# A decoder trunk on one core: dense matmuls read their moved operand from two halves in turn

## The chip, the cores and the metric

The kernel runs on one core of one Trainium2 chip. The metric is the device time of the program in microseconds (us), median of several runs; lower is better. Five engines work side by side and meet by semaphores: TensorE (PE: matmuls, and PEld: the loads of the operand that is held in the array), VectorE (DVE), ScalarE (ACT), GpSimd (POOL) and SyncE (SP, which here only issues DMAs). A matmul holds one operand of up to 128 x 128 in the array (the held one, loaded ahead) and streams the columns of the other past it (the moved one); its result goes to a bank of PSUM, 512 float32 in each of 128 partitions, of which there are eight. DVE and ACT take results out of PSUM into SBUF (here called an evacuation).

## The reference, cut to what matters

```python
for l in range(DEPTH):                       # 2 layers, x is 512 tokens x 1024
    x = x + 0.5 * swiglu(rms_norm(x, ffn1_norm[l]), ffn1_w_in[l], ffn1_w_out[l])
    h = rms_norm(x, mix_norm[l]) @ w_mix_in[l]            # 1024 -> 3336
    ...                                                   # conv, HGRN2 and forgetting attention
    x = x + y @ w_mix_out[l]                              # 1024 -> 1024
    x = x + 0.5 * swiglu(rms_norm(x, ffn2_norm[l]), ffn2_w_in[l], ffn2_w_out[l])

def swiglu(h, w_in, w_out):                               # 1024 -> 2 x 2816 -> 1024
    gate, up = jnp.split(h @ w_in, 2, axis=-1)
    return (jax.nn.silu(gate) * up) @ w_out
```

Everything is float32.

## The kernel before

**Three products for one.** Each float32 operand is split into a rounded part (`hi`) and a rest (`lo`), both of a four-byte type that PE streams in one pass; a product is hi x hi + hi x lo + lo x hi. `mm3` (L408 to 422) issues these three matmuls (L413, L419, L420). The weights are split as they arrive: an ACT cast writes `hi`, a DVE subtraction `lo` (L398 and L401 in `parted`, L865 and L867 in `prepare`), both into a tile `hl`. The activations stand ready as pairs: `xh`, `xl` (normalised input, made in `norm_part`), `hh`, `hl` (hidden values), `yh`, `yl` (mixer output).

**Two kinds of matmuls.** The larger part of each feed-forward block is computed by a seven-product scheme on halves of the tokens (`halved`, planned in `plan`); its matmuls move 256 columns and go through `mm3` too. The rest is dense and moves 512 columns: with the features in the rows of the result, the 512 tokens are moved past a 128 x 128 block of weights; with the tokens in the rows (`tokens`, and the last output chunk), 512 columns of weights are moved past 128 tokens. These dense stages are:

- the entry of each feed-forward block (`cover`, L651 on): the first `covered` blocks of hidden features (6 in the first block, 4 in the others), for which PE has work while the normalisation and the operands of the seven-product scheme are prepared. The preparing steps are dealt out by the table `ENTRY`;
- its last chunk of w_out (`ffn`, second half), 6 rows of blocks; in the very last block it is done with the tokens in the rows, and the last quarter of the output in two half-wide pieces;
- the mixer: `features` for the HGRN inputs, `tokens` for the attention's q, k, v (`fox_qkv`, L1528 on), `features_steps` for the convolution (`conv_in`, `conv_out`), and the output projection (`most`, then a loop over `dg`).

All of them go through `stream_steps` (L428 on), which walks over the rows of the weights, two or more blocks of 128 at a time, and calls `mm3` for each job (a bank, a slice of weights). Two places issue the three products themselves: the opening of the program (`first`, L466) and the last rows of the first half of the output projection (`late`, L497).

**Banks and order.** `next4` gives two sets of four banks in turn, so that one set is evacuated while the next is filled. The order of PE's instructions is written out by hand through `follow`; DVE and ACT keep program order in the stages where their work is dealt.

**The evacuations** of dense results: the residual additions (L644 in `ffn`; L1210 `add` in `mix`; L633 for the output), the multiplication by the inverse norm (L667, L668 `clear`; L1124, L1126, L1142 in `mix`; L1255, L1272 in the convolution), a copy (L1254), and in `fox_qkv` the copies of q and k (L1567) and the split of v (L1578, L1579). Each reads one bank in order.

Of the kernel before, what the change touches and what calls it, by code (L numbers as in the profile page):

```python
# [26 lines left out]
T = 512  # L27
# [39 lines left out]
HD = 64  # L67
# [12 lines left out]
def plan(covered):  # L80
# [89 lines left out]
    for a, b, what in sorted(loose, key=lambda x: (x[1], x[0])):  # L170
# [8 lines left out]
    return seq, {  # L179
        n: [(w[0], w[1:]) for _, w in sorted(todo[n], key=lambda x: x[0])] for n in todo  # L180
    }


class Trunk:
# [223 lines left out]
    def mm3(self, acc, ah, al, bh, bl, first, last, parted=False, keep=False):  # L408

        nc = self.nc  # L410
        n = bh.shape[-1]
        for c in (slice(0, n // 2), slice(n // 2, n)) if parted else (slice(0, n),):
            i = nc.tensor.matmul(  # L413
                acc[:, c], ah, bh[:, c], start=first and c.start == 0, stop=False,
                skip_group_check=True,
            )
            if keep:
                self.follow("p", i)
        nc.tensor.matmul(acc, ah, bl, start=False, stop=False, skip_group_check=True)  # L419
        i = nc.tensor.matmul(acc, al, bh, start=False, stop=last, skip_group_check=True)  # L420
        if keep:
            self.follow("p", i)

# [4 lines left out]
    def stream_steps(  # L428
        self, jobs, parts_of, act, nk, mid=None, pre=None, deal=None, keep=False, lead=False,
        fine=False, deep=2, rowwise=False, late=False,  # L430
    ):

        k = 0
        while k < nk:
            kk = min(deep, nk - k)
            if callable(mid) and k == nk - 2:
                mid()
            st = None  # L450
            if pre is not None:

                if k == 0:
                    st = self.open_rows(parts_of(k, kk), kk)
                pre(k)
            if deal is not None:
                deal(k)
            skew = SKEW_MOVING if jobs[0][2] is not None and jobs[0][0].shape[-1] < T else 0
            if st is not None:

                def first(hi, lo):

                    ah, al = act(0)
                    for n, (w, x) in enumerate(((hi, ah), (lo, ah), (hi, al))):
                        for acc, cols, _ in jobs:
                            self.follow("p", self.nc.tensor.matmul(  # L466
                                acc, w[:, cols], x, start=n == 0, stop=False, skip_group_check=True
                            ))
                        if n == 0:
                            pre(k, None)  # L470

                self.between = first
            rows = self.granule(parts_of(k, kk), kk, pre is None, skew, deal is not None, st)
            if st is not None:
                self.first_rows = self.chain["v"]
            end = k + kk == nk
            order = (
                [(job, j) for job in jobs for j in range(kk)]
                if end and not rowwise or lead and k == 0
                else [(job, j) for j in range(kk) for job in jobs]  # L480
            )
            for n, ((acc, cols, toks, *more), j) in enumerate(order):
                if pre is not None and n == len(order) // 2:
                    pre(k, True)
                if fine and n == len(order) // 2:
                    yield
                if pre is not None and k + j == 0:
                    continue
                ah, al = act(k + j)
                hi, lo = rows[j]  # L490
                first, stop = k + j == 0 and not more, end and j == kk - 1
                if late and stop:

                    if acc is jobs[0][0]:
                        for i, (w, x) in enumerate(((hi, ah), (lo, ah), (hi, al))):
                            for acc, cols, _ in jobs:
                                self.follow("p", self.nc.tensor.matmul(  # L497
                                    acc, w[:, cols], x, start=False, stop=i == 2, skip_group_check=True
                                ))
                    continue  # L500
                if toks is None:
                    self.mm3(acc, hi[:, cols], lo[:, cols], ah, al, first, stop, False, keep)
                else:
                    self.mm3(
                        acc, ah[:, toks], al[:, toks], hi[:, cols], lo[:, cols], first, stop, False, keep
                    )
            k += kk
            yield
# [74 lines left out]
    def ffn(self, w_in, w_out, next_gain, covered, mean=None, begin=None, out=None):  # L583
# [5 lines left out]
        with tc.tile_pool(name=self.n("ffn"), bufs=1) as fp:  # L589
# [14 lines left out]
            for dg in range(2):  # L604
# [24 lines left out]
                if last:  # L629
                    for i in range(4):  # L630
                        o = self.xo[dg * 4 + i]
                        for bk, c in pieces[i]:
                            nc.vector.scalar_tensor_tensor(  # L633
                                out=o[:, c], in0=bk, scalar=0.5,
                                in1=xs[dg * 4 + i][:, c], op0=ALU.mult, op1=ALU.add,
                            )
                            nc.sync.dma_start(
                                out[0, spans[i], dg * T + c.start : dg * T + c.stop], o[:, c]
                            )
                    continue  # L640
                for i in range(4):
                    j = dg * 4 + i
                    xj = self.xT[:, j, :]
                    nc.vector.scalar_tensor_tensor(  # L644
                        out=xj, in0=banks[i], scalar=0.5, in1=xj,
                        op0=ALU.mult, op1=ALU.add,
                    )
                    if next_gain is not None:
                        self.norm_part(j, fp)

    def cover(self, fp, w_in, w_out, covered, mean, begin):  # L651
# [10 lines left out]
        def clear(t):  # L662

            gi = fp.tile([P, T], F32, tag="g2", name=self.n("gi"), bufs=2)
            ui = fp.tile([P, T], F32, tag="u2", name=self.n("ui"), bufs=2)
            pg, pu = tiles[t]
            V(nc.vector.tensor_mul(gi, pg, self.inv))  # L667
            V(nc.vector.tensor_mul(ui, pu, self.inv))  # L668
            values[t] = gi, ui

        def value(t):
# [387 lines left out]
    def mix(self, l, w, w_out, conv_w, out_gain, q_gain, k_gain, f_bias, next_gain, logits):  # L1059
# [3 lines left out]
        with tc.tile_pool(name=self.n("mix"), bufs=1) as mp:  # L1063
# [48 lines left out]
            with tc.tile_pool(name=self.n("hg"), bufs=1) as hp:  # L1112
# [8 lines left out]
                inv = self.inv  # L1121
                z, sg = pair(hp, "z"), pair(hp, "sg")
                for i in range(2):
                    nc.vector.tensor_mul(z[i], bz[i], inv)  # L1124
                for i in range(2):
                    nc.vector.tensor_mul(sg[i], bg[i], inv)  # L1126
                self.table(SILU)
                for i in range(2):
                    self.act(sg[i], sg[i], AF.Silu)
# [9 lines left out]
                )  # L1139
                bq = features([(H_Q, 256)], ("mm", "mm"))  # L1140
                for i in range(2):
                    nc.vector.tensor_mul(q[i], bq[i], inv)  # L1142

                bv = [self.bank(t) for t in ("mm", "sc", "sc", "mm")]
                self.stream(
# [29 lines left out]
            with tc.tile_pool(name=self.n("at"), bufs=1) as ap_:  # L1175
# [31 lines left out]
                    return lambda k: (self.yh[order[k0 + k]], self.yl[order[k0 + k]])  # L1207

                def add(j, bank):
                    nc.vector.tensor_add(self.xT[:, j, :], bank, self.xT[:, j, :])  # L1210

                def most():

# [36 lines left out]
    def conv_in(self, pool, i, px, pc, inv2, cw):  # L1250
        nc = self.nc
        u = pool.tile([P, T], F32, tag="t", name=self.n("cu"), bufs=self.tb)
        y = self.mp.tile([P, T], F32, tag=f"cyl{i}", name=self.n("cy"))
        nc.scalar.copy(y, px)  # L1254
        nc.vector.tensor_mul(u, pc, inv2)  # L1255
        nc.vector.tensor_mul(u, u, y)
        tap = lambda j: cw[:, 2 * j + i : 2 * j + i + 1]
        nc.scalar.activation(y, u, AF.Copy, scale=tap(2))
        nc.vector.scalar_tensor_tensor(
            out=y[:, 1:], in0=u[:, : T - 1], scalar=tap(1), in1=y[:, 1:], op0=ALU.mult, op1=ALU.add  # L1260
        )
        nc.vector.scalar_tensor_tensor(
            out=y[:, 2:], in0=u[:, : T - 2], scalar=tap(0), in1=y[:, 2:], op0=ALU.mult, op1=ALU.add
        )
        self.cy = getattr(self, "cy", {})
        self.cy[i] = y

    def conv_out(self, pool, i, pb):
        nc = self.nc
        y = self.cy[i]  # L1270
        u = pool.tile([P, T], F32, tag="t", name=self.n("cu"), bufs=self.tb)
        nc.vector.tensor_mul(u, pb, self.inv)  # L1272
        nc.vector.tensor_mul(u, y, u)
        self.yl[i] = self.mp.tile([P, T], F32R, tag=f"cyl{i}", name=self.n("cyl"))
        nc.scalar.copy(self.yh[i], u)
# [252 lines left out]
    def fox_qkv(self, mp, hp, tokens, half):  # L1528
# [34 lines left out]
        for hf in range(2):  # L1563
            qk = mp.tile([P, 4, 4, 2, HD], F32, tag="qk", name=self.n("qk"), bufs=2)
            banks = yield from beside(tokens((F_Q + 256 * hf, 256), (F_K + 256 * hf, 256)))
            for i, bank in enumerate(banks):
                nc.scalar.copy(  # L1567
                    qk[:, i].rearrange("p h w d -> p w h d"),
                    bank.rearrange("p (w h d) -> p w h d", w=2, h=4),
                )  # L1570
                later.append(lambda qk=qk, i=i: norm(qk, i))
            half.append(qk)
        V = mp.tile([P, 4, NH, 2, HD], F32R, tag="V", name=self.n("V"))
        half.append(V)
        for i, bank in enumerate((yield from beside(tokens((F_V, T), keep=True)))):
            src = bank.rearrange("p (h d) -> p h d", d=HD)
            sc = self.invc[:, i : i + 1]
            nc.scalar.activation(V[:, i, :, 0, :], src, AF.Copy, scale=sc)  # L1578
            nc.vector.scalar_tensor_tensor(  # L1579
                out=V[:, i, :, 1, :], in0=src, scalar=sc, in1=V[:, i, :, 0, :],  # L1580
                op0=ALU.mult, op1=ALU.subtract,
            )

    def fox_prep(self, pool, h, qk, g):
# [280 lines left out]
```

## Time and profile before

| what | value |
|---|---|
| median of 3 runs | 1821.0 us (1819.95 to 1823.05) |
| profiled execution, span from first to last instruction | 1816.5 us |
| median of the runs above that span | 4.5 us |
| PE busy | 1808.4 us, 100% of the span |
| DVE busy | 1431.7 us, 79% |
| ACT busy | 995.2 us, 55% |
| share of PE in the chain that ended last | 96% |
| granted TensorE clock, mean | 1.000 |

The profile is of one execution, whose own duration is known as its span; what lies around the span is taken from the difference to the median of the runs. Busy times of PE overlap: each record reaches from a matmul's start to the modelled end of its last column. How fast a stream of matmuls runs is therefore read from the distance of their starts.

### The profile page before, as it was taken

The numbers are of one execution on the slowest core, as the hardware profiler recorded it, in microseconds if no ns is written. First come the engines' busy times: TensorE is split into PE (matmuls) and PEld (weight loads), VectorE is DVE, ScalarE is ACT, GpSimd is POOL, SyncE is SP. The second block draws the span as 40 slices with busy tenths as digits, with TensorE's granted clock in tenths as the row PEclk, the third lists the DMA queues.
The fourth block names the chain that finished last, engine by engine and source line by source line (L and its number), as shares of the span: only waits on it lengthen the run. The fifth ranks groups of instructions, "written<-read, shape, count | busy, mean of one in ns | idle before, by whom it ended". The sixth has DMA issues, their size and how long they took to land.

```text
span 1816.5 us, 33373 instructions
## 1 busy us (share of the span) xinstructions
PE 1808.4 (100%) x13613; PEld 1656.6 (91%) x13613; DVE 1431.7 (79%) x1991; ACT 995.2 (55%) x1417; POOL 176.8 (10%) x174
## 2 busy tenths in 40 slices
PE   9999999999999999999999999999999999999999
PEld 7899999887788899999889999998878888999998
DVE  8889887678677898879678887876777778888883
ACT  5455555465665465555445555555656655555552
POOL 0011120100000101112001111201000001020210
PEclk9999999999999999999999999999999999999999
DMA  7658784343543867868276787923435438677762
GB/s 214 180 128 191 182 174 97 73 115 87 129 106 99 225 141 160 196 161 170 82 202 141 165 190 188 172 66 82 122 84 126 118 96 217 163 153 197 152 139 93
DMA packets 253114, 262.35 MB, mean 144 GB/s; under 512 B 23528, under 2 KB 232176, under 8 KB 252960
## 3 DMA queue, kind: packets, MB, share of 16 engines
q1 hardware_dynamic: 197104, 192.02, 35.9%
q0 software_dynamic: 55840, 68.19, 23.5%
q8 instruction: 107, 1.75, 0.4%
q14 instruction: 47, 0.39, 0.1%
q10 hardware_dynamic: 16, 0.00, 0.0%
HBM read 226.15 MB, written 2.17 MB: 126 GB/s over the span
## 4 chain that ended last, share of the span: by engine, by line
PE 96%; DVE 1%; DMA 1%; ACT 1%; issue 0%; SPq 0%; ACTq 0%; DVEq 0%
PE mm L413 15%; PE mm L420 14%; PE mm L419 14%; PE sc L413 6%; PE sc L420 6%; PE sc L419 6%; PE pt L413 6%; PE pt L420 6%; PE pt L419 6%; PE po L413 4%; PE po L419 4%; PE po L420 4%; PE sc L1641 1%; PE po L1696 1%; PE pt L1678 1%; DMA st<-in_ffn_w_in_dram 1%
## 5 line engine op out<-in xcount | busy, mean ns | idle before, releaser
L865 ACT CAST hl<-w 128x1024 fp32r<-128x1024 f32 x322 | 337.7, 1050 | 348.3 <-PE mm L420 81.4
L867 DVE TENSOR_TENSOR hl<-w,hl 128x1024 fp32r<-128x1024 f32 x322 | 393.1, 1222 | 85.8 <-ACT hl L865 85.7
L401 DVE TENSOR_TENSOR hl<-st,hl 128x1024 fp32r<-128x1024 f32 (+3 forms) x152 | 160.3, 1054 | 122.0 <-ACT hl L398 121.5
L398 ACT CAST hl<-st 128x1024 fp32r<-128x1024 f32 (+3 forms) x151 | 138.3, 916 | 188.9 <-PE po L420 85.7
L413 PE MATMUL mm<-xc,hl 128*128 128x256 f32 (+1 forms) x730 | 201.6, 277 | 0.3 <-ACT g L964 0.3
L420 PE MATMUL mm<-xc,hl 128*128 128x256 f32 x728 | 201.6, 277 | 0.0
L419 PE MATMUL mm<-xc,hl 128*128 128x256 f32 x728 | 201.5, 277 | 0.0
L413 PE MATMUL sc<-xc,hl 128*128 128x256 f32 (+1 forms) x530 | 146.6, 277 | 0.6 <-ACT g L964 0.6
L420 PE MATMUL sc<-xc,hl 128*128 128x256 f32 x528 | 146.4, 277 | 0.0
L419 PE MATMUL sc<-xc,hl 128*128 128x256 f32 x528 | 146.2, 277 | 0.0
L413 PEld LDWEIGHTS mm<-xc,hl 128*128 128x128 f32 x730 | 137.1, 188 | 0.8 <-ACT g L964 0.5
L420 PEld LDWEIGHTS mm<-xc,hl 128*128 128x128 f32 x728 | 136.8, 188 | 0.2 <-DVE hl L867 0.2
L419 PEld LDWEIGHTS mm<-xc,hl 128*128 128x128 f32 x728 | 136.8, 188 | 0.0
L419 PE MATMUL pt<-xc,hl 128*128 128x256 f32 x480 | 132.9, 277 | 0.0
L413 PE MATMUL pt<-xc,hl 128*128 128x256 f32 (+1 forms) x482 | 132.9, 276 | 0.0
L420 PE MATMUL pt<-xc,hl 128*128 128x256 f32 x480 | 132.8, 277 | 0.0
L413 PE MATMUL mm<-x,hl 128*128 128x512 f32 x272 | 109.0, 401 | 0.0
L420 PE MATMUL mm<-x,hl 128*128 128x512 f32 x272 | 106.3, 391 | 0.0
L419 PE MATMUL mm<-x,hl 128*128 128x512 f32 x272 | 106.0, 390 | 0.0
L413 PEld LDWEIGHTS sc<-xc,hl 128*128 128x128 f32 x530 | 99.6, 188 | 1.5 <-ACT g L964 1.0
L420 PEld LDWEIGHTS sc<-xc,hl 128*128 128x128 f32 x528 | 99.2, 188 | 0.1
L419 PEld LDWEIGHTS sc<-xc,hl 128*128 128x128 f32 x528 | 99.2, 188 | 0.0
(506 smaller groups left out, 5431.6 us busy)
## 6 DMA issues: line engine op xcount, KB each, us to landing
w<-in_ffn_w_in_dram SPq DMA_DIRECT2D x140, 512.0 KB, 6.6
w<-in_ffn_w_out_dram SPq DMA_DIRECT2D x64, 512.0 KB, 5.4
w<-in_ffn_w_out_dram POOLq DMA_DIRECT2D x56, 512.0 KB, 9.4
st<-in_w_mix_in_dram SPq DMA_DIRECT2D x80, 256.0 KB, 3.0
w<-in_ffn_w_in_dram POOLq DMA_DIRECT2D x39, 512.0 KB, 8.7
st<-in_ffn_w_in_dram SPq DMA_DIRECT2D x70, 256.0 KB, 4.4
w<-S POOLq DMA_DIRECT2D x35, 512.0 KB, 4.8
st<-in_ffn_w_out_dram SPq DMA_DIRECT2D x24, 512.0 KB, 3.9
```

What stands on the lines that cost most here:

```text
L398: a = nc.scalar.copy(hi, src[:, c : c + w])
L401: b = nc.vector.tensor_sub(lo, src[:, c : c + w], hi)
L413: i = nc.tensor.matmul(acc[:, c], ah, bh[:, c], start=first and c.start == 0, stop=False, skip_group_check=True,)
L419: nc.tensor.matmul(acc, ah, bl, start=False, stop=False, skip_group_check=True)
L420: i = nc.tensor.matmul(acc, al, bh, start=False, stop=last, skip_group_check=True)
L865: A(nc.scalar.copy(hi, src))
L867: return lambda: V(nc.vector.tensor_sub(lo, src, hi))
L1641: mm = lambda *a, **k: E(nc.tensor.matmul(*a, skip_group_check=True, **k))
L1678: E(nc.tensor.transpose(tb[:, k * P : (k + 1) * P], to[u][:, j * P : (j + 1) * P], self.ident))
L1696: E(nc.tensor.matmul(self.ob[:, o], half[2][:, j, h].rearrange("p a d -> p (a d)"), part[:, at[0] : at[-1] + 1, :].rearrange("p b t -> p ( ...
```

## The change

In every matmul whose moved operand is 512 columns wide, that operand is given in another order: column 0, column 256, column 1, column 257 and so on, which is an access pattern of two steps, the inner one of 256 elements (1024 bytes), the outer one of one element. Column 2t + h of the bank then belongs to element 256h + t. Operands of 256 or 264 columns are read as before. The evacuations of these banks read PSUM with a step of two elements, first all even columns, then all odd ones, and write the values where they stood before. Held operands, weights, DMAs, buffers and the order of the instructions stay as they are.

```diff
+def woven(x):
+    return x.rearrange("p (h t) -> p t h", h=2) if x.shape[-1] == T else x
+
+def halves(x):
+    return x.rearrange("p (h t) -> p h t", h=2)
+
+def unwoven(bank):
+    return bank.rearrange("p (t h) -> p h t", h=2)
...
             i = nc.tensor.matmul(
-                acc[:, c], ah, bh[:, c], start=first and c.start == 0, stop=False,
+                acc[:, c], ah, woven(bh[:, c]), start=first and c.start == 0, stop=False,
                 skip_group_check=True,
             )
...
-        nc.tensor.matmul(acc, ah, bl, start=False, stop=False, skip_group_check=True)
-        i = nc.tensor.matmul(acc, al, bh, start=False, stop=last, skip_group_check=True)
+        nc.tensor.matmul(acc, ah, woven(bl), start=False, stop=False, skip_group_check=True)
+        i = nc.tensor.matmul(acc, al, woven(bh), start=False, stop=last, skip_group_check=True)
...
                     nc.vector.scalar_tensor_tensor(
-                        out=xj, in0=banks[i], scalar=0.5, in1=xj,
+                        out=halves(xj), in0=unwoven(banks[i]), scalar=0.5, in1=halves(xj),
                         op0=ALU.mult, op1=ALU.add,
                     )
...
-            V(nc.vector.tensor_mul(gi, pg, self.inv))
-            V(nc.vector.tensor_mul(ui, pu, self.inv))
+            for v, bank in ((gi, pg), (ui, pu)):
+                V(nc.vector.tensor_mul(halves(v), unwoven(bank), halves(self.inv)))
...
                 nc.scalar.copy(
                     qk[:, i].rearrange("p h w d -> p w h d"),
-                    bank.rearrange("p (w h d) -> p w h d", w=2, h=4),
+                    bank.rearrange("p (h d w) -> p w h d", w=2, h=4),
                 )
...
-            src = bank.rearrange("p (h d) -> p h d", d=HD)
+            src = bank.rearrange("p (h d w) -> p w h d", w=2, d=HD)
             sc = self.invc[:, i : i + 1]
-            nc.scalar.activation(V[:, i, :, 0, :], src, AF.Copy, scale=sc)
+            vh, vl = (V[:, i, :, a, :].rearrange("p (w h) d -> p w h d", w=2) for a in range(2))
+            nc.scalar.activation(vh, src, AF.Copy, scale=sc)
```

The two other places that issue the three products (`first`, `late`) weave in the same way, and the other evacuations listed above are rewritten like L644 and L667. In the last output chunk the two half-wide pieces are read in order, in two halves (`unwoven(bk) if whole else halves(bk)`).

More of the change, by code (lines that the diff above doesn't have):

```diff
@@ L466, in first @@
                             self.follow("p", self.nc.tensor.matmul(
-                                acc, w[:, cols], x, start=n == 0, stop=False, skip_group_check=True
+                                acc, w[:, cols], woven(x), start=n == 0, stop=False, skip_group_check=True
                             ))
@@ L497, in stream_steps @@
                                 self.follow("p", self.nc.tensor.matmul(
-                                    acc, w[:, cols], x, start=False, stop=i == 2, skip_group_check=True
+                                    acc, w[:, cols], woven(x), start=False, stop=i == 2, skip_group_check=True
                                 ))
@@ L632, in ffn @@
                         for bk, c in pieces[i]:
+                            whole = c.stop - c.start == T
                             nc.vector.scalar_tensor_tensor(
-                                out=o[:, c], in0=bk, scalar=0.5,
-                                in1=xs[dg * 4 + i][:, c], op0=ALU.mult, op1=ALU.add,
+                                out=halves(o[:, c]), in0=unwoven(bk) if whole else halves(bk),
+                                scalar=0.5, in1=halves(xs[dg * 4 + i][:, c]),
+                                op0=ALU.mult, op1=ALU.add,
                             )
@@ L1123, in mix @@
                 for i in range(2):
-                    nc.vector.tensor_mul(z[i], bz[i], inv)
+                    nc.vector.tensor_mul(halves(z[i]), unwoven(bz[i]), halves(inv))
                 for i in range(2):
-                    nc.vector.tensor_mul(sg[i], bg[i], inv)
+                    nc.vector.tensor_mul(halves(sg[i]), unwoven(bg[i]), halves(inv))
                 self.table(SILU)
@@ L1141, in mix @@
                 for i in range(2):
-                    nc.vector.tensor_mul(q[i], bq[i], inv)
+                    nc.vector.tensor_mul(halves(q[i]), unwoven(bq[i]), halves(inv))
                 bv = [self.bank(t) for t in ("mm", "sc", "sc", "mm")]
@@ L1209, in add @@
                 def add(j, bank):
-                    nc.vector.tensor_add(self.xT[:, j, :], bank, self.xT[:, j, :])
+                    xj = halves(self.xT[:, j, :])
+                    nc.vector.tensor_add(xj, unwoven(bank), xj)
                 def most():
@@ L1253, in conv_in @@
         y = self.mp.tile([P, T], F32, tag=f"cyl{i}", name=self.n("cy"))
-        nc.scalar.copy(y, px)
-        nc.vector.tensor_mul(u, pc, inv2)
+        nc.scalar.copy(halves(y), unwoven(px))
+        nc.vector.tensor_mul(halves(u), unwoven(pc), halves(inv2))
         nc.vector.tensor_mul(u, u, y)
@@ L1271, in conv_out @@
         u = pool.tile([P, T], F32, tag="t", name=self.n("cu"), bufs=self.tb)
-        nc.vector.tensor_mul(u, pb, self.inv)
+        nc.vector.tensor_mul(halves(u), unwoven(pb), halves(self.inv))
         nc.vector.tensor_mul(u, y, u)
@@ L1575, in fox_qkv @@
         for i, bank in enumerate((yield from beside(tokens((F_V, T), keep=True)))):
-            src = bank.rearrange("p (h d) -> p h d", d=HD)
+            src = bank.rearrange("p (h d w) -> p w h d", w=2, d=HD)
             sc = self.invc[:, i : i + 1]
-            nc.scalar.activation(V[:, i, :, 0, :], src, AF.Copy, scale=sc)
+            vh, vl = (V[:, i, :, a, :].rearrange("p (w h) d -> p w h d", w=2) for a in range(2))
+            nc.scalar.activation(vh, src, AF.Copy, scale=sc)
             nc.vector.scalar_tensor_tensor(
-                out=V[:, i, :, 1, :], in0=src, scalar=sc, in1=V[:, i, :, 0, :],
-                op0=ALU.mult, op1=ALU.subtract,
+                out=vl, in0=src, scalar=sc, in1=vh, op0=ALU.mult, op1=ALU.subtract
             )
```

## The prediction

> **What bounds the kernel now.** The head of the page, its busy line of PE and the chain of work that ended last come first. They tell whether a change to a matmul can move the end at all.
>
> ```profile
> span 1816.5 us, 33373 instructions
> PE 1808.4 (100%) x13613; PEld 1656.6 (91%) x13613; DVE 1431.7 (79%) x1991; ACT 995.2 (55%) x1417; POOL 176.8 (10%) x174
> ...
> PE 96%; DVE 1%; DMA 1%; ACT 1%; issue 0%; SPq 0%; ACTq 0%; DVEq 0%
> ```
>
> PE works or has work in flight through the whole span, and 96% of the chain is PE. What the change does to the time from one matmul to the next goes to the end almost whole; what it does to DVE or ACT counts only where their work comes late for PE. Busy time of PE isn't its rate, though: records overlap. The rate is read from the starts in the timeline. First eight dense matmuls of 512 columns, then sixteen of 256 columns (first and last of each row of them):
>
> ```profile
> 611.79 0.39 PE L413 MATMUL mm<-x,hl 128*128 128x512 f32 x1
> ...
> 613.37 0.39 PE L419 MATMUL po<-x,hl 128*128 128x512 f32 x1
> ```
> ```profile
> 199.79 0.28 PE L413 MATMUL sc<-m,hl 128*128 128x256 f32 x1
> ...
> 201.49 0.28 PE L413 MATMUL mm<-xc,hl 128*128 128x256 f32 x1
> ```
>
> Seven steps in 1.58 us are 226 ns for 512 columns; fifteen steps in 1.70 us are 113 ns for 256. The two are in the ratio of the columns, 0.442 ns a column, with no fixed part for an instruction. So a steady stream of such matmuls is paced column by column. The durations say the same (group list of the page, and grouped by form):
>
> ```profile
> L420 PE MATMUL mm<-xc,hl 128*128 128x256 f32 x728 | 201.6, 277 | 0.0
> L420 PE MATMUL mm<-x,hl 128*128 128x512 f32 x272 | 106.3, 391 | 0.0
> ```
> ```profile
> L1641 PE MATMUL sc<-maskb,identb 128*128 128x128 bf16 x32 | 7.4, 232 | 0.0
> L1641 PE MATMUL sc<-maskb,identb 128*128 128x256 bf16 x16 | 4.5, 284 | 0.0
> ```
>
> Here 256 more columns of four bytes cost 391 - 277 = 114 ns, 0.445 a column; 128 more columns of two bytes cost 284 - 232 = 52 ns, 0.406 a column. The array can therefore take a column in about 0.41 ns, and four-byte columns arrive some 9% slower. What limits them looks like the reading of the moved operand. That is the one thing which the change touches on PE.
>
> **The change, part by part.**
>
> *Which matmuls.* Only operands whose last axis is 512 are woven. Counted from the loops: entries (the `cover` loop) 288 + 3 x 192 = 864; last chunks 3 x 144 + 126 = 558 (the final one has two half-wide jobs, 18 matmuls, left as they are); mixers 2 x 768 = 1536. Together 2958, at 226 ns about 669 us of the span. The 8740 of 256 columns keep their reading, and no weight load, DMA, wait or queue order is moved.
>
> *What a woven read costs.* The same 512 elements of a partition are read, but each column lies 1024 bytes from the one before it, in turn forth and back. No matmul in this trace reads so; its cost is bounded from the nearest rows. Downward: if the pace of 0.442 is a stall of one running stream, which a second stream can fill, the floor is the two-byte pace, 512 x 0.406 = 208 ns, 18 ns less than now. Upward: rows of ACT show what jumping reads can cost. L1423 reads SBUF with a step of 32 bytes; L1254 reads in order; L1353 reads PSUM with a step of 256 bytes.
>
> ```profile
> L1423 ACT COPY lk<-S 128x448 f32<-128x448 f32 x4 | 4.2, 1054 | 0.0
> L1353 ACT COPY t<-pt 128x256 f32<-128x256 f32 x8 | 2.7, 388 | 4.2 <-PE pt L1347 4.2
> L1485 ACT COPY t<-sc 128x256 f32<-128x256 f32 x4 | 1.6, 394 | 0.0
> ```
> ```profile
> L1254 ACT COPY cy<-mm x4: 579/584/587, 483.6 to 1399.3; 128x512 f32<-128x512 f32 x4
> ```
>
> In order, ACT needs (584 - 394)/256 = 0.74 ns an element and some 204 ns once; with the step of 32 bytes (1054 - 204)/448 = 1.90 ns, 2.6 times as much. At 1.90 ns a column a woven matmul would take 973 ns; at 2.6 times PE's own pace 588 ns; at one lost slot for each column 2 x 226 = 452 ns. But L1423 never returns to a neighbour of what it has read; the woven read does so at every second column, each half in order. Which of the two it resembles, no row shows.
>
> I take 216 ns, 10 ns less than now: somewhat over half of the 18, because the two-byte slope is 52 ns read to 1 ns (0.398 to 0.414 a column) and leaves out what each instruction may cost once. That is 2958 x 10 = 30 us less on PE. The ends kept for the range are 208 ns (53 us less) and 973 ns.
>
> The Trainium skill (TensorE: Matmul & The Clock Gate, "Wait — 56ns, not 53.3ns?") gives 215.7 ns from start to start for 512 columns of bf16 on a warm clock. By an estimate from that page the saving would be 2958 x 10.3 = 30 us; for four-byte columns the trace has its own 226.
>
> *The evacuations.* About 130 DVE operations of 512 elements and 28 ACT ones now read PSUM with a step of 8 bytes and walk the two halves in turn; outputs and second inputs stay in order within each half. ACT's L1353 above reads PSUM with a step 32 times as wide at 388 ns, against 394 for L1485 in order: nothing. DVE's L1379 steps by 8 bytes on all three of its SBUF operands, 256 elements each; L644 and L867 run in order:
>
> ```profile
> L1379 DVE TENSOR_TENSOR t<-t,q x4: 399/410/419, 404.4 to 1302.0; 128x256 f32<-128x256 f32 x4
> ```
> ```profile
> L644 DVE SCALAR_TENSOR_TENSOR xT<-pt,xT 128x512 f32<-128x512 f32 x6 | 4.1, 683 | 0.0
> L867 DVE TENSOR_TENSOR hl<-w,hl 128x1024 fp32r<-128x1024 f32 x322 | 393.1, 1222 | 85.8 <-ACT hl L865 85.7
> ```
>
> In order DVE needs (1222 - 683)/512 = 1.05 ns an element, which makes 683 - 256 x 1.05 = 414 ns for 256 elements; L1379 takes 410. I cost the step at nothing. Its upper bound is ACT's factor: 2.6 times the 512 x 1.05 = 538 ns, 0.86 us more for each, 112 us of DVE in all. Most of it would lie in DVE's idle 21%; PE goes on with the other set of four banks. Where that cover is missing, at some fourteen ends of a stage whose result feeds the next norm, it would be about 1 us each, 14 us.
>
> *What is late next.* Less time on PE asks the same casts sooner. Two stretches of dense matmuls (us, then busy us of each engine):
>
> ```profile
> 310.00:345.00 35.00, 35.00 (x156) 28.97 (x156) 20.49 (x30) 15.15 (x23) 0.00 (x0) 1.00 0.27 78
> ...
> 606.00:628.00 22.00, 22.00 (x99) 18.24 (x98) 21.87 (x32) 10.17 (x11) 1.54 (x2) 1.00 0.92 261
> ```
>
> In the first DVE has 14 us of air; in the second, the end of an entry, 21.87 of 22 us are DVE's, while DMA is at 0.92. Four such ends of 22 us can't get 4.4% faster: 4 us of the 30 are lost there. The entry's dealt work (`ENTRY`) then comes late for the products behind it.
>
> *Sum.* 30 - 4 = 26 us, against the profiled span 1816.5 - 26 = 1790.5; the median of the runs shown, 1821.0, lies 4.5 above that span. Forecast: **1795 us**.
>
> **The rivals.**
>
> *Two streams defeat the reading (slower).* If PE's read port works best while consecutive columns lie side by side, and keeps only the last place open, each woven column costs a fresh access. It decides from the first nanosecond over 226, at each of the 2958 matmuls in all dense stages; a single lost slot a column gives 2958 x 226 = 669 us more, 2490 us (at the two-byte slot, 2 x 208 = 416 ns, 2383). For it: the ACT row, and that four-byte columns are already slower than two-byte ones, so the reading has no air. Against it: each half is read in order, and every neighbourhood is wanted again one column later. Its worse form, 588 to 973 ns, gives 2892 to 4031 us.
>
> The Trainium skill (SBUF — State Buffer, "Door 1: The DMA port swizzle") speaks for this rival: SBUF is read in lines of 16 bytes, full bandwidth needs at least two consecutive accesses to one line, and every crossing pays. Four fp32 share such a line; the woven read crosses at each column. L1423's 1.90 ns agrees with it for ACT; for PE no row does.
>
> *Nothing changes.* If the pace is one of bytes, 512 x 4 at 9 bytes a ns, the order doesn't matter: 226 ns stays and the end at 1821, or up to 14 us later if DVE pays for the step. For it: exact proportion to columns. Against: a port that cares for bytes alone would not give L1423 its 1.90 ns.
>
> *The gain is eaten.* PE is faster but DVE, at 79% and 99% at entries' ends, holds it: with DVE's step at its upper bound, 14 us of the 26 go, 1809 us.
>
> That the compiler undoes the weave is excluded: 1024 bytes of step can't be merged into one run.
>
> **How the numbers follow.** The asymmetry is plain: at best 18 ns of 226 are to be had, at worst hundreds are lost. Still the trace shows that the array can go faster than its feed, and a second stream is what would fill a stall. Chances: the forecast, with 1768 to 1815 as its own range and the eaten gain in it, 0.48; unchanged within 0.2% 0.05, and up to 14 us slower 0.03; a lost slot a column, 2383 to 2490, 0.26; the worse form 0.18. The range that leaves out only the last is 1768 to 2500, 0.82 of the cases. Faster by over 0.2% 0.48, within 0.2% (about what a measurement of this kernel can tell from no change) 0.05, slower 0.47.
>
> **What would show it.** In the timeline, the starts of eight steady L413/L419/L420 matmuls of 512 columns: 7 steps in 1.51 us for the forecast, 1.58 for no change, 3 us or more for the rival; those of 256 columns must stay at 113 ns. DVE's L644 and L667 counterparts at 683 ns show the step free; over 0.75 us would not. DVE's share in the entries' ends, and waits of PE on `hl` in them, show the eaten part. The forecast is wrong if the step is over 226 ns, and the sum is wrong if PE waits on DVE for more than 4 us in all.

## The result and the profile after

| | before | after |
|---|---|---|
| median of the runs (4 each, on one chip) | 1820.47 us (1818.09 to 1823.05) | **1789.44 us** (1787.50 to 1790.36) |
| ratio, 95% interval | 1 | 0.9831 (0.9818 to 0.9845) |
| profiled execution, span | 1816.5 us | 1785.7 us |
| PE busy within the span | 1808.4 us | 1774.0 us |
| PE idle within the span | 8.1 us | 11.7 us |

The change takes 31.0 us off the median; the span shrinks by 30.8, which is 34.4 us less PE work and 3.6 us more PE idle time. The forecast was 1795 us. The code that the new lines name is the old one, 15 to 18 lines further down (L413, L419, L420 are now L428, L434, L435; L644 and L667 are L661 and L685).

The head of the page of after, its busy line and its chain by engine:

```profile
span 1785.7 us, 33379 instructions
PE 1774.0 (99%) x13613; PEld 1659.7 (93%) x13613; DVE 1428.7 (80%) x1991; ACT 993.9 (56%) x1417; POOL 176.8 (10%) x174
...
PE 87%; DVE 6%; ACT 4%; DMA 2%; issue 1%; SPq 0%; ACTq 0%; DVEq 0%
```

The same 13613 matmuls; DVE and ACT are as busy as before, within 3 us. In the chain PE fell from 96% to 87%: with a faster PE, the chain followed back from the end runs more often over DVE and ACT. The pace is read from starts again. First and last of eight dense matmuls of 512 columns (timeline of after: start us, us, engine, line, operation):

```profile
592.64 0.38 PE L428 MATMUL sc<-x,hl 128*128 128x512 f32 x1
...
594.15 0.38 PE L434 MATMUL pt<-x,hl 128*128 128x512 f32 x1
```

Seven steps in 1.51 us, **216 ns** each where 226 ns were. The group rows of the page agree: 512 columns take 379 ns instead of 391, while 256 columns stay where they were (276 ns, 277 before).

```profile
L435 PE MATMUL mm<-xc,hl 128*128 128x256 f32 x728 | 201.2, 276 | 0.0
L435 PE MATMUL mm<-x,hl 128*128 128x512 f32 x272 | 103.1, 379 | 0.0
```

Between first and last start, the seven-product stages take the same time as before (228.72 and 228.72 us, 248.6 and 249.0, 248.7 and 248.6, 248.7 and 248.7). The five dense stretches between them shrink from 77.5 to 75.0, 322.6 to 311.6, 77.4 to 73.7, 322.6 to 310.4 and 36.5 to 35.0 us: 30.9 us together, the whole difference.

The evacuations, now with a step of two in PSUM (groups by form: busy us, mean ns):

```profile
L661 DVE SCALAR_TENSOR_TENSOR xT<-pt,xT 128x512 f32<-128x512 f32 x6 | 4.1, 682 | 0.0
L685 DVE TENSOR_TENSOR gi<-pt,inv 128x512 f32<-128x512 f32 x5 | 3.4, 683 | 0.0
L1228 DVE TENSOR_TENSOR xT<-mm,xT 128x512 f32<-128x512 f32 x22 | 14.7, 682 | 4.2 <-PE mm L435 4.2
```

They take what L644 took in order, 683 ns. ACT's copy of a bank (L1254 before, L1272 now) takes 584 ns in both. Two stretches of after that answer to those of the prediction (window, its length, then busy us and count of PE, PEld, DVE, ACT, POOL; clock, DMA share, GB/s):

```profile
305.00:338.00 33.00, 33.00 (x156) 28.71 (x155) 18.60 (x27) 13.08 (x19) 0.00 (x0) 1.00 0.27 83
593.00:615.00 22.00, 22.00 (x104) 19.26 (x103) 21.81 (x32) 10.77 (x11) 1.28 (x1) 1.00 0.97 282
```

In the first, 156 matmuls start in 33 us instead of 35. The second is the end of an entry: 104 matmuls start in 22 us instead of 99, with DVE as full as before (21.81 of 22 us) and the DMA share at 0.97; PE's 512-column matmuls in it start 215.8 ns apart in the mean. Where PE waits now (waits of PE in after: total us, times, longest us):

```profile
PE sc L1659 <- ACT P L324: 1.7, 4, 0.6
...
PE mm L428 <- DVE q L1159: 0.9, 1, 0.9
...
PE sc L1659 <- issue: 0.5, 2, 0.3
PE sc L512 <- ACT fyh L1731: 0.5, 2, 0.2
```

Of these, the trace of before has only the first, with 0.4 us. Together that is 3.2 us more than before, of 3.6 us of new idle time, and all of it lies in the mixers: attention's softmax results `P`, the scaled `q`, the products behind `fyh`. None of it is a wait for `hl` in an entry.

### The profile page after: what moved, and what is told of

It reads as the page before. It is cut to its first block, busy times and chain, and to the rows that moved or that the text cites. A ratio compares the mean times of both kernels' runs of the same rounds, so it can differ in the third digit from the quotient of the medians.

```text
span 1785.7 us, 33379 instructions
## 1 busy us (share of the span) xinstructions
PE 1774.0 (99%) x13613; PEld 1659.7 (93%) x13613; DVE 1428.7 (80%) x1991; ACT 993.9 (56%) x1417; POOL 176.8 (10%) x174
## 4 chain that ended last, share of the span: by engine, by line
PE 87%; DVE 6%; ACT 4%; DMA 2%; issue 1%; SPq 0%; ACTq 0%; DVEq 0%
PE mm L428 13%; PE mm L435 12%; PE mm L434 12%; PE sc L428 6%; PE sc L435 6%; PE sc L434 6%; PE pt L428 6%; PE pt L434 6%; PE pt L435 6%; PE po L428 3%; PE po L434 3%; PE po L435 3%; DVE hl L416 2%; ACT hl L413 1%; DMA st<-in_ffn_w_in_dram 1%
## 5 line engine op out<-in xcount | busy, mean ns | idle before, releaser
L413 ACT CAST hl<-st 128x1024 fp32r<-128x1024 f32 (+3 forms) x151 | 137.7, 912 | 166.3 <-PE po L435 78.4
L428 PE MATMUL mm<-xc,hl 128*128 128x256 f32 (+1 forms) x730 | 201.3, 276 | 0.3 <-ACT g L981 0.3
L435 PE MATMUL mm<-xc,hl 128*128 128x256 f32 x728 | 201.2, 276 | 0.0
L434 PE MATMUL mm<-xc,hl 128*128 128x256 f32 x728 | 201.1, 276 | 0.0
L428 PE MATMUL sc<-xc,hl 128*128 128x256 f32 (+1 forms) x530 | 146.4, 277 | 0.6 <-ACT g L981 0.6
L435 PE MATMUL sc<-xc,hl 128*128 128x256 f32 x528 | 146.1, 277 | 0.1
L434 PE MATMUL sc<-xc,hl 128*128 128x256 f32 x528 | 146.0, 277 | 0.0
L428 PEld LDWEIGHTS mm<-xc,hl 128*128 128x128 f32 x730 | 137.1, 188 | 0.8 <-ACT g L981 0.5
L435 PEld LDWEIGHTS mm<-xc,hl 128*128 128x128 f32 x728 | 136.7, 188 | 0.1
L434 PEld LDWEIGHTS mm<-xc,hl 128*128 128x128 f32 x728 | 136.7, 188 | 0.0
L434 PE MATMUL pt<-xc,hl 128*128 128x256 f32 x480 | 132.6, 276 | 0.0
L428 PE MATMUL pt<-xc,hl 128*128 128x256 f32 (+1 forms) x482 | 132.6, 276 | 0.0
L435 PE MATMUL pt<-xc,hl 128*128 128x256 f32 x480 | 132.5, 276 | 0.0
L428 PE MATMUL mm<-x,hl 128*128 128x512 f32 x272 | 105.9, 389 | 0.0
L435 PE MATMUL mm<-x,hl 128*128 128x512 f32 x272 | 103.1, 379 | 0.0
L434 PE MATMUL mm<-x,hl 128*128 128x512 f32 x272 | 103.1, 379 | 0.0
L428 PEld LDWEIGHTS sc<-xc,hl 128*128 128x128 f32 x530 | 99.5, 188 | 1.4 <-ACT g L981 1.0
L435 PEld LDWEIGHTS sc<-xc,hl 128*128 128x128 f32 x528 | 99.2, 188 | 0.3 <-DVE hl L884 0.3
L434 PEld LDWEIGHTS sc<-xc,hl 128*128 128x128 f32 x528 | 99.1, 188 | 0.0
```

The lines of the kernel that those rows point to most:

```text
L413: a = nc.scalar.copy(hi, src[:, c : c + w])
L428: i = nc.tensor.matmul(acc[:, c], ah, woven(bh[:, c]), start=first and c.start == 0, stop=False, skip_group_check=True,)
L434: nc.tensor.matmul(acc, ah, woven(bl), start=False, stop=False, skip_group_check=True)
L435: i = nc.tensor.matmul(acc, al, woven(bh), start=False, stop=last, skip_group_check=True)
```

## The experiments

The time is explained by a pace. What stays open is why: the prediction took the two far halves for two streams, of which the second fills the stalls of the first. The experiments read the moved columns in other orders. Each is the changed kernel with another `woven`; where the order differs from the change's, the evacuations put the columns back as the change does, so results come out permuted, as the expectation says. The times of 2 to 10 are of one execution each, those of 1, 11 and 12 medians of ten, five and four. "Pace" is the median distance of the starts of 512-column matmuls.

**1. The evacuations alone**

```diff
 def woven(x):
-    return x.rearrange("p (h t) -> p t h", h=2) if x.shape[-1] == T else x
+    return x
```

> The moved operands are read in order again, the evacuations keep their step of two in PSUM (so the columns of the dense results are permuted). Theory, the whole gain is the pace of the 2958 matmuls: 226 ns from start to start as before, DVE evacuations at 680 to 690 ns, time 1820.5 us, ratio 1.000 to before. Rival, the stepped evacuations change something themselves: ratio off 1.000 by more than 0.002, either way.

Measured: 1819.15 us, ratio to before 1.0003 (0.9993 to 1.0013). The group by form in this run:

```profile
L435 PE MATMUL mm<-x,hl 128*128 128x512 f32 x272 | 106.1, 390 | 0.0
```

The pace is back at 226 to 227 ns and the time at that of before: the step in PSUM costs and brings nothing, and the whole gain is in the order in which PE reads.

**2. Two halves of every 32 bytes instead of two halves of the row** (columns 0, 4, 1, 5, 2, 6, 3, 7)

```diff
-    return x.rearrange("p (h t) -> p t h", h=2) if x.shape[-1] == T else x
+    return x.rearrange("p (n h r) -> p n r h", h=2, r=4) if x.shape[-1] == T else x
```

> The same kind of order with a small distance: of every 8 columns 0, 4, 1, 5, 2, 6, 3, 7, so each column lies 16 bytes from the one before it, in turn forth and back (results permuted). Theory, the two places have to be far apart (two long streams): 226 ns stays, about 1820 us. Rival, it is enough that consecutive columns lie 16 bytes apart, in neighbouring lines: 216 ns, about 1789 us. A third: neighbours collide and it is slower than 226 ns.

Measured: 1789.88 us. Ten steps in the timeline:

```profile
592.52 0.38 PE L434 MATMUL sc<-x,hl 128*128 128x512 f32 x1
...
594.68 0.38 PE L435 MATMUL sc<-x,hl 128*128 128x512 f32 x1
```

216 ns a step, all of the gain with a distance of 16 bytes where the change has 1024. That the halves lie far apart isn't needed; the theory that asked for it falls.

**3. Runs of four columns from each half in turn** (0 to 3, 256 to 259, 4 to 7, ...)

```diff
+    return x.rearrange("p (h n r) -> p n h r", h=2, r=4) if x.shape[-1] == T else x
```

> Halves in turn, but four columns (16 bytes) from each before the other (results permuted). Theory, what is lost in one running stream is lost between its pieces, and any turn between two far places fills it: 216 ns, about 1789 us. Rival, the turn must come at every column: 226 ns, about 1820 us.

Measured: 1880.87 us. Ten steps:

```profile
624.75 0.42 PE L428 MATMUL sc<-x,hl 128*128 128x512 f32 x1
...
627.25 0.42 PE L434 MATMUL pt<-x,hl 128*128 128x512 f32 x1
```

250 ns a step (246 and 254 in turn), slower than in order. Neither expectation holds (216 ns, 226 ns): two far halves in turn don't help of themselves.

**4. The 256-column matmuls woven too** (the halves then 512 bytes apart)

```diff
+    return x.rearrange("p (h t) -> p t h", h=2) if x.shape[-1] in (T, T // 2) else x
```

> The 8740 matmuls of 256 columns are woven too, from halves of 128 columns, 512 bytes apart (results permuted, their evacuations are not adapted). Theory, their pace of 113 ns is the same stall: 108 ns, 8740 x 5.4 = 47 us less, about 1742 us if DVE and ACT keep up. Rival, 256 columns are bound by the load of the held operand or by DVE's casts: 113 ns stays, 1789 us.

Measured: 1775.62 us. Seven products of three matmuls:

```profile
198.03 0.28 PE L428 MATMUL mm<-xc,hl 128*128 128x256 f32 x1
...
200.38 0.28 PE L428 MATMUL pt<-m,hl 128*128 128x256 f32 x1
```

2.35 us for 21 steps, 112 ns each (111 to 112 over the run), from 113. Half of the 512-column pace would be 108: the weave brings these only some 1.5 ns of the 5, and the time lies between the two that were expected. Something else holds them at 111 to 112; experiment 10 asks what.

**5 and 6. One column of every 16 bytes, one of every 8 bytes**

```diff
+    return x.rearrange("p (n r) -> p r n", r=4) if x.shape[-1] == T else x   # 5
+    return x.rearrange("p (n r) -> p r n", r=2) if x.shape[-1] == T else x   # 6
```

> The 512 columns in four passes with a step of 16 bytes: 0, 4, 8 ... 508, then 1, 5, 9 ... (results permuted). No line of 16 bytes is visited twice within 128 columns. Theory A, what costs time is that successive columns lie in the same 16 bytes, and PE needs no second place kept open: 216 ns, about 1789 us. Theory B, two places are kept open and a return within two columns is needed: every column is a new place, 416 to 973 ns, 2380 us or more.

> Even columns, then odd ones: a step of 8 bytes, two successive columns in each 16 bytes (results permuted). Theory A: between the two, some 221 ns, about 1805 us; or 216 if two in a place are few enough. Theory B: a place is used twice before it is left, 226 ns or more, 1819 us or more.

Measured: 2502.09 and 2477.76 us. Four steps of the first, ten of the second:

```profile
708.93 0.66 PE L434 MATMUL mm<-x,hl 128*128 128x512 f32 x1
...
710.77 0.66 PE L435 MATMUL mm<-x,hl 128*128 128x512 f32 x1
```
```profile
713.62 0.65 PE L434 MATMUL mm<-x,hl 128*128 128x512 f32 x1
...
718.15 0.64 PE L435 MATMUL mm<-x,hl 128*128 128x512 f32 x1
```

460 and 453 ns a step, twice the 226 ns in order. With the step of 16 bytes theory A falls and theory B is borne out: an order that takes one column and doesn't come back to its neighbours soon costs a slot for each column. For the step of 8 bytes A's 221 ns fell, and B had named only a lower bound. That it is hardly better, though two columns in succession come from one 16 bytes, is the clue for the theory below.

**7. The order turned within 16 bytes** (0, 2, 1, 3)

```diff
+    return x.rearrange("p (n a b) -> p n b a", a=2, b=2) if x.shape[-1] == T else x
```

> The order is changed inside each 16 bytes alone: 0, 2, 1, 3, then 4, 6, 5, 7 (results permuted). Theory A, four successive columns still lie in one place: 226 ns, 1819 us. Rival, any departure from unit steps gives 216 ns, 1789 us: what costs is the unit step itself.

Measured: 1821.24 us, ten steps of 226 ns:

```profile
624.34 0.39 PE L434 MATMUL mm<-x,hl 128*128 128x512 f32 x1
...
626.60 0.39 PE L435 MATMUL po<-x,hl 128*128 128x512 f32 x1
```

An order that differs from the plain one only within 16 bytes changes nothing.

**8 and 9. Runs of two from each half, and four quarters in turn**

```diff
+    return x.rearrange("p (h n r) -> p n h r", h=2, r=2) if x.shape[-1] == T else x   # 8
+    return x.rearrange("p (h t) -> p t h", h=4) if x.shape[-1] == T else x            # 9
```

> Halves in turn, but two columns (8 bytes) from each before the other (results permuted). Runs of four took 246 to 254 ns, runs of one 216. Theory A: two successive columns in one place, between the two, 225 to 235 ns, 1815 to 1845 us. Rival, a jump costs a fixed time whatever the run: twice the jumps of runs of four, 275 ns or more, 1960 us.

> Four quarters in turn: 0, 128, 256, 384, 1, 129 ... (results permuted). Theory S, formed from the runs before: even and odd places of the order are read by two streams of their own, and each stream is fast while it stays in the same 16 bytes; here each stream changes its place at every column (0, 256, 1, 257 ... and 128, 384, 129, 385 ...), as in runs of two: about 333 ns, 2130 us. Rival, any turn between distant places that comes at every column fills the stall: 216 ns, 1789 us.

Measured: 2127.71 and 1977.53 us. Six steps of the first, five of the second:

```profile
629.60 0.50 PE L435 MATMUL mm<-hy,hl 128*128 128x512 f32 x1
...
631.60 0.50 PE L435 MATMUL mm<-hy,hl 128*128 128x512 f32 x1
```
```profile
629.43 0.45 PE L428 MATMUL mm<-cyh,hl 128*128 128x512 f32 x1
...
630.85 0.45 PE L435 MATMUL mm<-fyh,hl 128*128 128x512 f32 x1
```

333 and 284 ns. For runs of two, the 225 to 235 ns of theory A fell; the rival had only "275 or more". Both are slower than in order, and the quarters, which differ from the change only in being four instead of two, lose 67 ns where the halves win 10. The quarters' size was missed: some 333 ns were expected.

**What the orders have in common.** Sort the columns by their place in the reading order, even places and odd places, and ask how many columns in a row each of these two streams takes out of one aligned 16 bytes (four columns):

| order of reading | a stream takes from 16 bytes | pace, ns |
|---|---|---|
| halves (the change); halves of 32 bytes (2) | 4 in a row | 216 |
| in order (before, 1); 0, 2, 1, 3 (7) | 2 in a row, then the next 16 bytes | 226 to 227 |
| runs of 4 (3) | 2 in a row, then a jump | 246 to 254 |
| quarters (9) | 1, and back to it after one other, 3 times | 283 |
| runs of 2 (8) | 1, and back to it after one other, once | 333 |
| step 8 bytes (6), step 16 bytes (5) | 1, no return | 451, 461 |

This theory, **S**, puts the groups of the nine orders in the measured sequence. It doesn't give the sizes (why a jump costs some 24 ns more than the next 16 bytes, why returning helps as much as it does), and it doesn't tell the steps of 8 and 16 bytes apart. It was formed after the other orders had been measured; the one that it forecast, the quarters, came out 50 ns off. It is inferred from times, as a way to sort them: no view shows two streams, and that PE reads so is not shown.

**10. What holds the 256-column matmuls at 111 ns.** As 4, with the second and third matmul of each product only 240 columns wide:

```diff
+    return x.rearrange("p (h t) -> p t h", h=2) if x.shape[-1] in (T, T // 2, 240) else x
...
+        m = slice(0, 240 if n == T // 2 else n)
-        nc.tensor.matmul(acc, ah, woven(bl), start=False, stop=False, skip_group_check=True)
-        i = nc.tensor.matmul(acc, al, woven(bh), start=False, stop=last, skip_group_check=True)
+        nc.tensor.matmul(acc[:, m], ah, woven(bl[:, m]), start=False, stop=False, skip_group_check=True)
+        i = nc.tensor.matmul(acc[:, m], al, woven(bh[:, m]), start=False, stop=last, skip_group_check=True)
```

> The matmuls of 256 columns are woven from halves of 128 as in the run that wove them too, and the second and third matmul of each three move 240 columns alone (part of two products is left out, results permuted). If the load of the held operand sets their 111 ns: 111 ns for 240 columns as well, about 1776 us. If the moved columns set it: 104 ns after those of 240, 5820 x 7 = 41 us less, about 1735 us.

Measured: 1789.41 us. One product and the start of the next in the timeline, then the waits of PE:

```profile
199.89 0.28 PE L428 MATMUL pt<-m,hl 128*128 128x256 f32 x1
200.01 0.27 PE L435 MATMUL pt<-m,hl 128*128 128x240 f32 x1
200.11 0.28 PE L436 MATMUL pt<-m,hl 128*128 128x240 f32 x1
200.22 0.28 PE L428 MATMUL pt<-m,hl 128*128 128x256 f32 x1
```
```profile
PE mm L436 <- DVE hl L887: 4.0, 3, 3.6
PE po L436 <- DVE hl L887: 3.7, 1, 3.7
PE pt L436 <- DVE hl L887: 3.0, 1, 3.0
```

A product takes 0.33 us from first to first start, 335 ns in the median of the run (steps of 118, 105 and 112 ns); in experiment 4 it takes 335 as well. Thirty-two columns fewer save nothing, so columns don't set this pace. What is left for each matmul is the load of the held 128 x 128 block, one for each of the 13613. The edit didn't vary that load, but the trace of before has matmuls with another one (timeline of before; the L1641 matmul and `PL` both move 128 columns, the first past a held block of two-byte elements, the second of four-byte ones):

```profile
485.08 0.23 PE L1641 MATMUL sc<-maskb,identb 128*128 128x128 bf16 x1
485.12 0.37 PE L1696 MATMUL po<-PH,V 128*128 128x256 f32 x1
...
485.50 0.27 PE L1696 MATMUL po<-PL,V 128*128 128x128 f32 x1
485.62 0.45 PE L413 MATMUL mm<-x,hl 128*128 128x512 f32 x1
```

Behind the first kind the next matmul starts after 40 ns (median of the 32), behind the second after 110 (107 to 114 in all 32), although 128 four-byte columns alone would ask for 57 (an estimate, a quarter of 226). (`PH` before it, with 128 columns too, is followed after 59 to 66: there the load for `PL` had begun at its own start.) The loads show the same: the next load starts 6 ns behind that of a two-byte block (median), and 107 or more behind that of a four-byte one, in all but 11 of 12347 cases. So neither the columns nor the instruction takes 110 ns; the load of a four-byte block does, and the woven 256 columns start only some 2 ns further apart.

The total is 14 us above that of experiment 4 although the pace is the same: 10.7 us are the waits above, for split weights, each total nearly all of one long wait. The splits came late because DVE, which works in program order, stood before them for a small DMA (waits of DVE in this run):

```profile
DVE ngain L785 <- DMA gain<-in_ffn_norm_dram: 13.4, 3, 4.7
```

In experiment 4 DVE waited 1.2 us there. Behind two of PE's three long waits the granted clock is 0.50 for 3.4 us (windows 846.00:849.40 and 1170.30:1173.60), which by an estimate costs another 3.4 us. Why `gain` landed late in this one execution stays open.

**11. All matmuls woven, moved operands stored even columns first.** The 256-column operands of the seven-product scheme are written by `two` with all even columns first, so that the woven reading gives them in their order. ACT and DVE read their source with a step of 8 bytes for it:

```diff
 def two(self, hi, lo, src, other):
+    hi, lo = (x.rearrange("p k (h t) -> p h k t", h=2) for x in (hi, lo))
+    src = src.rearrange("p k (t h) -> p h k t", h=2)
...
     return nc.scalar.copy(hi, src), nc.vector.tensor_sub(lo, src, hi)
```

(The one DVE operation with a scalar there is issued in two halves, and `woven` is that of experiment 4.) The two half-wide pieces of the last quarter of the output stay in the woven order.

> The whole computation with the matmuls of 256 columns woven too: their moved operands are stored with even columns first, so that their results come out in order; the two operations that store them read with a step of 8 bytes. The 8740 matmuls go from 113 to 111 ns: 1775 us if DVE and ACT pay nothing for the step, ratio 0.975 to before; some 15 us of DVE (half the 60 splits need two operations in place of one) may cost up to 5 us. Rival, ACT pays for its step as L1423 did, the operands come late and PE waits: over 1789 us.

Measured: 1780.26 us, ratio to before 0.9786 (0.9773 to 0.9799). The groups by form of the stored operands, in this run and then in before:

```profile
L827 ACT CAST m<-hq 128x1024 fp32r<-128x1024 f32 x32 | 43.6, 1364 | 3.2 <-DVE hq L904 3.2
L827 DVE TENSOR_TENSOR m<-hq,m 128x1024 fp32r<-128x1024 f32 x32 | 43.2, 1349 | 10.2 <-ACT m L827 10.2
```
```profile
L803 DVE TENSOR_TENSOR m<-hq,m 128x1024 fp32r<-128x1024 f32 x32 | 39.1, 1223 | 4.9 <-ACT m L803 4.8
L803 ACT CAST m<-hq 128x1024 fp32r<-128x1024 f32 x32 | 33.4, 1044 | 2.8 <-DVE hq L880 2.8
```

ACT pays 0.32 us for each cast that reads SBUF with a step of 8 bytes, DVE 0.13; 4.6 us of what experiment 4 gained are gone again. It is faster than both kernels, but with its last pieces left in the woven order it isn't a whole kernel.

**12. The same with everything put back, ACT writing in turn.** The last quarter's pieces are evacuated in two halves as well, and ACT reads in order and writes to the two halves in turn, 512 bytes apart:

```diff
 def two(self, hi, lo, src, other):
+    turns = hi.rearrange("p k (h t) -> p k t h", h=2), src.rearrange("p k (t h) -> p k t h", h=2)
...
+    return nc.scalar.copy(*turns), nc.vector.tensor_sub(lo, src, hi)
```

> As the run before with all matmuls woven, with two differences: the last quarter of the output, in two pieces of 256 columns, is put back in order (the run before left that out), and ACT, which took 1364 to 1540 ns for a split where it read with a step of 8 bytes against 1044 in order, now reads in order and writes in turn to two halves 512 bytes apart. If ACT's writes take a step at no cost, as those of L1353 did: ACT back at 1.05 us, 1776 to 1780 us, ratio 0.977. Rival, writing in turn costs ACT as much as reading with a step or more: 1780 to 1790 us.

Measured: 1794.14 us, ratio to before 0.9864 (0.9847 to 0.9880). A group by form, then the longest wait of PE:

```profile
L827 ACT CAST m<-hq 128x1024 fp32r<-128x1024 f32 x32 | 66.0, 2064 | 3.2 <-DVE hq L904 3.2
```
```profile
PE sc L429 <- ACT g L988: 5.0, 2, 2.5
```

The expectation failed, and the time lies above its rival's too: ACT takes 2.06 us instead of 1.04, and PE waits 5.0 us for ACT's `g` where it waited 0.6 in before and 2.6 in experiment 11. The span is 13.5 us longer than there; 7.5 us of that are PE idle time, and what the other 6.0 are stays open. So the best whole version that was run is the change itself. Experiment 11 with its last pieces put back wasn't run.

## Why the prediction was right, point by point

- **PE bounds, so pace goes to the end.** Right: dense stretches lost 30.9 us, the total 31.0.
- **2958 matmuls at 10 ns.** The pace was taken at 216 ns and is 216. That it hits to the nanosecond is partly luck: the rows bounded it between 208 and 226, and where it lies between them was a choice. The term of 30 us came out as 34.4: before, starts did not keep to 226 ns after each interruption, but most of the next five distances were 229 to 237 (mean of all distances under 240 ns: 227.8); after, nearly all lie at 215 to 216 (mean 215.8). 2958 x 11.9 = 35 us. The steady eight matmuls from which 226 was read were the better end of the old pace.
- **Why it gets faster.** The picture, a stalling stream beside which a second one runs, forecast the time; its reason was half right. The prediction offered two far halves as the second stream; experiment 2 has the whole gain without distance, 3 and 9 have two or four far streams and are slower than in order. What the runs fit is S, inferred and not shown: how many columns each of the alternate places takes from one 16 bytes before it moves on.
- **The rival of a lost slot a column.** Its price was real, its place wrong: 452 ns were worked out, and the steps of 16 and 8 bytes cost 461 and 451 (2502 and 2478 us, where the rival had 2490). The woven read differs in the one thing that the prediction named against it: it comes back to each neighbourhood one column later.
- **The line rule.** The Trainium skill (SBUF — State Buffer, "Door 1: The DMA port swizzle") asks for at least two consecutive accesses to one line of 16 bytes. By consecutive columns the woven order never has two, and it is the fastest of all; the measurement decides against that reading of the rule for PE. Counted for each of the two alternate streams, the measured times come nearer to it: one column from a line 451 to 461 ns, two 226, four 216. But two are then not yet the fastest, and two with a jump between lines cost 246 to 254.
- **The evacuations at nothing.** Right: 682 to 683 ns, and experiment 1 alone at 1.0003 of before. The eaten gain had no cause.
- **4 us lost at the entries' ends.** Wrong: 104 matmuls instead of 99 fit in 22 us with DVE as full as before. That DVE was 99% busy there didn't mean that PE waited for it: the row showed a full engine, not a wait. The loss came elsewhere, 3.6 us of idle time, 3.2 of them in the mixers, where PE's chain runs through ACT and DVE; that its size is near 4 is chance. The sum, 26 us against the 30.8 by which the span shrank, is short by 4.4 us of PE work and 0.4 of idle time.
- **The signs.** The pace, the 256 columns and the evacuations came as the forecast asked. One sign against the sum showed: PE's waits on DVE add up to 4.4 us (3.0 before), over the limit of 4. They are not why the sum missed; that was PE's old pace, above.

## What to carry to other kernels

Where PE bounds and its 512-column matmuls of four-byte operands start 226 ns apart rather than 216, try the order in which the moved columns are read: it costs nothing on PE, and reading PSUM back with a step of 8 bytes was free for DVE and ACT here. Choose an order in which every second column stays in one aligned 16 bytes for four turns; halves of the row do, and halves of 32 bytes too. Quarters, runs and steps do not, and can double the time of a matmul. Before a loss is put down to a full engine, look for the wait that it causes.

## What the runs showed of the hardware

- PE's pace for 512 four-byte columns ranges from 216 to 461 ns with the order alone (table above), at the same bytes and a granted clock of 0.997 to 1.000.
- Woven matmuls of 256 columns stay at 111 to 112 ns when 32 of a product's 768 columns are dropped (335 ns for three, experiments 4 and 10), and four-byte loads of a 128 x 128 block start at least 107 ns apart in all but 11 of 12347 cases (before), also where a matmul moves 128 columns alone: the limit is then the load of the block, not the columns.
- Behind a wait of PE of 3.0 and one of 3.6 us the granted clock is 0.50 for 3.4 us; behind one of 3.7 us it stays at 1.00 (experiment 10).
- ACT pays more for a step in SBUF than DVE: a cast of 1024 elements takes 1044 ns in order, 1364 to read with a step of 8 bytes, 2064 to write in turn 512 bytes apart; DVE's subtraction 1223 in order and 1349 with the step. The same step of 8 bytes on a PSUM bank costs DVE nothing (682 to 683 ns) and ACT nothing (584 ns).
